# MLPs and output projections with 512-wide moving weights and stationary activations

## The chip, the cores and the metric

One core of a Trainium2 chip runs the whole kernel. The metric is the device time of one execution in microseconds (us). The kernel before was timed three times: 2537.08, 2537.50 and 2537.93 us, median 2537.5 us. The profile was taken from one more execution.

## What is computed

A trunk of two layers on 256 tokens of 2048 channels, all float32 (`SEQ = 256`, `D_MODEL = 2048`, `D_FF = 8192`). Cut to what this change touches:

```python
def squared_relu_mlp(h, w_up, w_down):
    u = h @ w_up                              # 2048 -> 8192
    return jnp.square(jax.nn.relu(u)) @ w_down  # 8192 -> 2048

# layer 0: attention and state-space heads share one input projection, then
x = x + concat([y_attn, y_ssd]) @ w_out       # 2048 -> 2048
x = x + squared_relu_mlp(rms_norm(x), w_up[0], w_down[0])
# layer 1: RWKV-7 time mixing, r, k, v projections and a scan over the tokens, then
x = x + (y * g) @ w_o                         # 2048 -> 2048
x = x + squared_relu_mlp(rms_norm(x), w_up[1], w_down[1])
```

Every large product is computed to float32 accuracy from two rounded halves of each operand: with x = xh + xl and w = wh + wl it is xh wh + xl wh + xh wl.

## The kernel before

**Layout.** The residual stream has channels on partitions: `x[d]` is [128 channels, 256 tokens], d = 0 to 15. The operand of a projection, `SA` or `SB`, is [128, 16, 512]: for each of 16 tiles of input channels (k) 256 columns of the rounded half and 256 of the rest.

**A unit** (`unit`, L372) is 128 outputs of a product with 2048 inputs. Its weights come in two loads of 512 KB (8 k tiles of 128x128 each; a load with its two halves is called a part below). ACT writes the rounded half `hi`, DVE the rest `lo`, three buffers each. Then TensorE makes two matmuls for each k, both with a tile of the weights as the stationary operand (`lhsT`): `hi` against all 512 columns of `X[:, k]`, `lo` against the first 256. The sum stands in one PSUM bank `pu` (two in turn) as two halves of 256 columns, which a reader adds.

**The MLP** (`mlp`, L515) makes 16 units of the up projection for a quarter c of the hidden channels, squares them into the other operand tile (ACT and DVE: `eb`, `u`, `uw`, `ut`, `split`), and then 16 units of the down projection, which DVE adds to `x[d]` in two steps. That is done for c = 0 to 3. 1/rms of the tokens multiplies `u`; it is made from squares that are summed over the tiles in `acc`, by matmuls and eleven short DVE steps (`token_rstd`). The last three tiles of the down projection of layer 0 (`'end': 3`) are left to the next stage (`mixer1_in`, steps `rest`).

**Output projections.** The first half of `w_out` (the attention heads) for 7 of the 16 tiles (`'early': 7`) and the first half of `w_o` for all 16 tiles (`o0a` to `o15a` in `PRM['order']`), and its second half for three of them (`+0a` to `+2a`), are multiplied within the mixers, among the work of the heads. There `feed` (L426) issues them: three matmuls of 256 columns for each k, again with the weights stationary. What is left follows in `out_proj` (L1029), which adds with DVE (`xT<-xT,pu`) and, for `w_o`, with POOL what the mixer had made of the first half (`xT<-xT,RY`).

**What sets the order.** Within the mixers a planner (`Streams`) issues the operations of many short programs in the order in which its rough costs let them start. In `out_proj` and `mlp` the framework's own scheduler orders the instructions of every engine. On the chip each engine works its list in order; loads of weights are issued by SP, the moves of the residual stream (`xd`, `out`) by POOL.

Of the kernel before, what the change touches and what calls it, by code (L numbers as in the profile page):

```python
# [97 lines left out]
def _heads(v):  # L98
    """a column to a head, on the first 64 partitions"""
    return np.concatenate([v.reshape(-1, HD).T, np.zeros((HD, D // HD), np.float32)], 0)  # L100


def layout(inp):
    a = {k: np.asarray(v) for k, v in inp.items()}
    o = {}
    o["xT"] = np.ascontiguousarray(a["x"][0].T.reshape(NK, P, L).transpose(1, 0, 2))
# [13 lines left out]
    o["w_out"] = _units(a["ev_w_out"][0][orow])  # L120
    for l in range(2):
        o[f"w_up{l}"] = _units(a["w_up"][l])
        o[f"w_dn{l}"] = np.ascontiguousarray(
            a["w_down"][l].reshape(4, NK, P, NK, P).transpose(0, 3, 2, 1, 4))
    for n in ("w_r", "w_k", "w_v", "w_o"):
        o[n] = _units(a["od_" + n][0])
    o["w1"] = np.ascontiguousarray(a["od_w1"][0].reshape(NK, P, 96).transpose(1, 0, 2))
# [31 lines left out]
# ---------------------------------------------------------------- interleaving  # L159
# [31 lines left out]
PRM = {'order': ['l0a', 'v0a', 'v0b', 'l1a', 'k3a', 'k3b', 'v1a', 'v1b', 'l2a', 'k4a', 'k4b', 'k5a', 'k5b', 'k6a', 'l3a', 'v2a', 'v2b', 'k6b', 'k7a', 'k7b', 'v3a', 'l4a', 'k8a', 'v3b', 'k8b', 'v4a', 'l5a', 'v4b', 'k9a', 'v5a', 'k9b', 'l6a', 'v5b', 'k10a', 'k10b', 'v6a', 'l7a', 'v6b', 'k11a', 'k11b', 'v7a', 'l8a', 'v7b', 'k12a', 'v8a', 'l9a', 'v8b', 'k12b', 'v9a', 'v9b', 'k13a', 'k13b', 'l10a', 'k14a', 'k14b', 'v10a', 'v10b', 'l11a', 'k15a', 'k15b', 'v11a', 'l12a', 'v11b', 'v12a', 'l13a', 'v12b', 'o0a', 'l14a', 'o1a', 'v13a', 'v13b', 'v14a', 'v14b', 'l15a', 'o2a', 'o3a', 'o4a', 'o5a', 'o6a', 'o7a', 'v15a', 'v15b', 'o8a', 'o9a', 'o10a', 'o11a', 'o12a', 'o13a', 'o14a', '+0a', '+1a', '+2a', 'o15a'], 'diff': 1.244, 'pool': 1000.0, 'b1p': 0.04, 'end': 3, 'step2': 1, 'w_blocks': -0.744, 'lat0P': 0.227, 'order0': [0, 12, 1, 2, 13, 14, 3, 4, 5, 15, 16, 24, 6, 17, 25, 7, 18, 19, 8, 20, 9, 21, 22, 26, 27, 10, 11, 23, 28, 29, 30, 31], 'm_attn1': -0.099, 'early': 7, 'm_gate': 0.043, 'm_norm_lo': 0.079, 'm_ssd': -0.022, 'pr': [3, 4], 'hid': [4, 7, 10], 'step1': 4, 'w_split_l': 0.571}  # L191
ORDER = 'v0a v0b l0a l1a k3a k3b v1a l2a v1b k4a k4b k5a k5b v2a l3a v2b k6a k6b k7a k7b v3a l4a v3b k8a k8b v4a l5a v4b k9a k9b v5a l6a v5b k10a k10b v6a l7a v6b k11a k11b v7a l8a v7b k12a k12b v8a l9a v8b k13a k13b v9a l10a v9b k14a k14b v10a l11a v10b k15a k15b v11a l12a v11b v12a l13a v12b o0a v13a l14a v13b o1a v14a l15a v14b o2a o3a v15a v15b o4a o5a o6a o7a o8a o9a o10a o11a o12a o13a o14a o15a +0a +1a +2a +3a'
ORDER = ORDER.split()

# [94 lines left out]
class Part:  # L289
    """Some k tiles of a unit, a 128-wide output tile of a projection. tiles: where the halves of the  # L290
    weights come to stand if the feed shall only split them; ready: the events that X[:, k] (the tiles) wait for"""
    def __init__(self, unit, h, src, X=None, n=8, m=P, k0=0, end=16, tiles=None, ready=None, bank=None):
        self.unit, self.key, self.src, self.X, self.n, self.m = unit, unit + (h,), src, X, n, m
        self.k0, self.end, self.tiles, self.ready, self.bank = k0, end, tiles, ready, bank


class Turns:
    """Tiles of a pool, n to a name, in turn"""
# [11 lines left out]
# ---------------------------------------------------------------- the program  # L310

class Trunk:
# [4 lines left out]
    # -- small helpers ---------------------------------------------------  # L317
# [24 lines left out]
    def mm(self, out, lhsT, rhs, start=True, stop=True):  # L342
        return self.nc.tensor.matmul(out, lhsT, rhs, start=start, stop=stop)  # L343
# [8 lines left out]
    def split(self, dst, src):  # L352
        """dst F32R [.., 512]: the rounded value and what it leaves, exactly"""
# [3 lines left out]
    def rsqrt(self, pool, v, shape, tag):  # L357
        """v f32 SBUF (any compact shape) -> 1/sqrt(v), Newton from the exponent trick"""
# [11 lines left out]
    # -- a 128-wide output tile of x @ W: [128, 512] in PSUM, the sum of its  # L370
# [1351 lines left out]
```

## Time and profile before

| what | value |
|---|---|
| median of three runs | 2537.5 us |
| span of the profiled execution | 2551.5 us |
| TensorE (PE) busy | 2477.5 us, 97% |
| weight loads (PEld) busy | 2181.3 us, 85% |
| DVE, ACT, POOL busy | 68%, 51%, 21% |
| memory traffic, mean | 163 GB/s |
| projection of layer 0 | from about 309 us |
| MLP of layer 0 | about 382 to 1106 us |
| r, k, v and the scan of layer 1 | about 1106 to 1757 us |
| rest of `w_o`, then MLP of layer 1 | about 1757 to 1817 us, then to 2547 us |

The profiled execution took 14 us (0.55%) longer than the median of the runs; its own rows are used for durations. In a timeline row the first number is the start in us from the span's start, the second how long it took; "x2" are two instructions merged into one row; in brackets stands how long the engine was idle before and which instruction released it. A matmul's own duration contains the time in which it drains through the array, so durations of neighbours overlap; the distance from start to start tells the rate.

### The profile page before, as it was taken

Reading aid. Unit: us, or ns where it says so; the run is one execution under the profiler, and the core shown is the slowest. Engines: PE = TensorE matmul, PEld = TensorE weight load, DVE = VectorE, ACT = ScalarE, POOL = GpSimd, SP = SyncE. Lnnn points to the kernel's source line nnn. Section 1 sums busy time; section 2 is a strip of 40 time slices with the busy share of each in tenths; the row PEclk is TensorE's granted clock in tenths of the full one; section 3 lists DMA queues with packets and bytes.
Section 4 is the critical chain, followed back from the end, with each engine's and each line's share of the span. In section 5 each row is a group of like instructions: output and inputs, shape, how many; then the busy total and the mean of one; then the engine's idle time right before and its main releaser. Section 6 shows DMA issues by size and latency. Waiting matters only on the chain. (4 is left out here: it accounts for less than half of the span.)

```text
span 2551.5 us, 45990 instructions
## 1 busy us (share of the span) xinstructions
PE 2477.5 (97%) x17612; PEld 2181.3 (85%) x17612; DVE 1738.2 (68%) x3287; ACT 1306.5 (51%) x2398; POOL 527.2 (21%) x933
## 2 busy tenths in 40 slices
PE   8999999999999999979999999999899999999999
PEld 7988988888888888879998888788688888888887
DVE  7888876656656656679876767667665565665665
ACT  5455555435445345556656566555453453453543
POOL 3443200000000000046455656552200000000000
PEclk9999999999999999989999999899999999999999
DMA  5433455555555555634442323334455555555554
GB/s 193 141 108 109 151 187 182 187 185 188 184 189 184 188 184 188 209 113 164 162 153 93 108 95 106 97 108 171 145 190 186 187 184 188 185 188 185 189 194 162
DMA packets 130348, 415.27 MB, mean 163 GB/s; under 512 B 23600, under 2 KB 26288, under 8 KB 130128
## 3 DMA queue, kind: packets, MB, share of 16 engines
q1 hardware_dynamic: 128160, 406.44, 46.9%
q0 software_dynamic: 1968, 5.90, 0.6%
q8 instruction: 138, 2.26, 0.3%
q14 instruction: 82, 0.67, 0.1%
HBM read 407.56 MB, written 4.72 MB: 162 GB/s over the span
## 5 line engine op out<-in xcount | busy, mean ns | idle before, releaser
L322 DVE TENSOR_TENSOR lo<-wt,hi 128x1024 fp32r<-128x1024 f32 (+2 forms) x895 | 937.4, 1054 | 529.6 <-ACT hi L319 511.8
L319 ACT ACTIVATE hi<-wt 128x1024 fp32r<-128x1024 f32 (+2 forms) x945 | 813.6, 873 | 818.3 <-PE pu L343 786.7
L343 PE MATMUL pu<-SA,hi 128*128 128x512 f32 (+2 forms) x4184 | 1162.0, 349 | 18.2 <-ACT SA L319 8.0
L343 PE MATMUL pu<-SB,hi 128*128 128x512 f32 (+2 forms) x3304 | 1003.1, 366 | 4.0 <-POOL SB L322 2.2
L343 PE MATMUL pu<-SA,lo 128*128 128x256 f32 (+1 forms) x3168 | 895.8, 283 | 0.3 <-DVE lo L322 0.3
L343 PEld LDWEIGHTS pu<-SA,hi 128*128 128x128 f32 (+1 forms) x4184 | 724.8, 191 | 135.2 <-ACT hi L319 9.7
L343 PE MATMUL pu<-SB,lo 128*128 128x256 f32 x2752 | 775.7, 282 | 1.7 <-DVE lo L322 1.6
L343 PEld LDWEIGHTS pu<-SB,hi 128*128 128x128 f32 (+1 forms) x3304 | 587.0, 190 | 115.6 <-POOL SB L322 2.6
L343 PEld LDWEIGHTS pu<-SA,lo 128*128 128x128 f32 (+1 forms) x3168 | 603.6, 191 | 1.2 <-DVE lo L322 0.5
L343 PEld LDWEIGHTS pu<-SB,lo 128*128 128x128 f32 x2752 | 522.6, 190 | 2.5 <-DVE lo L322 2.3
L1694 POOL DMA_DIRECT2D out<-xT x16 | 8.7, 544 | 708.0 <-DVE xT L322 708.0
L1661 POOL DMA_DIRECT2D xd<-xh x13 | 7.2, 554 | 696.5 <-DVE xh L322 696.5
L322 DVE TENSOR_TENSOR xh<-xh,pu 128x256 f32<-128x256 f32 x164 | 69.2, 422 | 53.7 <-PE pu L343 51.1
L322 DVE TENSOR_TENSOR xT<-xT,pu 128x256 f32<-128x256 f32 x154 | 64.8, 421 | 47.9 <-PE pu L343 45.3
L322 POOL TENSOR_TENSOR lo<-wt,hi 128x512 fp32r<-128x512 f32 (+1 forms) x50 | 69.1, 1387 | 66.3 <-ACT hi L319 62.2
L322 POOL TENSOR_TENSOR xt<-Nb,X 128x60 f32<-128x60 f32 (+14 forms) x240 | 74.7, 311 | 28.4 <-DMA Nb<-dn 12.1
L322 POOL TENSOR_TENSOR X<-X,xt 128x60 f32<-128x60 f32 (+14 forms) x240 | 74.2, 309 | 16.4
L319 ACT ACTIVATE uv<-ps_c,n 64x64 f32<-64x64 f32 x128 | 39.5, 309 | 53.0 <-PE ps_c L343 40.3
L322 POOL TENSOR_TENSOR SB<-st,SB 128x256 fp32r<-128x256 f32 x44 | 49.3, 1135 | 43.8 <-ACT SB L319 31.4
L340 DVE SCALAR_TENSOR_TENSOR uw<-u,rb 128x256 f32<-128x256 f32 x128 | 54.5, 425 | 4.4
L340 DVE SCALAR_TENSOR_TENSOR st<-dx,vec,xh 128x256 f32<-128x256 f32 x80 | 53.3, 700 | 2.0 <-POOL SB L322 2.0
L322 DVE TENSOR_TENSOR u<-pu,eb 128x256 f32<-128x256 f32 x128 | 53.6, 418 | 0.0
(310 smaller groups left out, 2073.2 us busy)
## 6 DMA issues: line engine op xcount, KB each, us to landing
wt<-in_w_up SPq DMA_DIRECT2D x256, 512.0 KB
wt<-in_w_dn SPq DMA_DIRECT2D x256, 512.0 KB
wt<-in_w_in SPq DMA_DIRECT2D x64, 512.0 KB
wt<-in_w_out SPq DMA_DIRECT2D x32, 512.0 KB
wt<-in_w_k SPq DMA_DIRECT2D x32, 512.0 KB
wt<-in_w_v SPq DMA_DIRECT2D x32, 512.0 KB
wt<-in_w_o SPq DMA_DIRECT2D x32, 512.0 KB
wt<-in_w_r SPq DMA_DIRECT2D x26, 512.0 KB
```

The source lines that it names most:

```text
L319: return self.nc.scalar.activation(out=out, in_=in_, func=func, **kw)
L322: return (eng or self.nc.vector).tensor_tensor(out=out, in0=a, in1=b, op=op)
L340: return self.nc.vector.scalar_tensor_tensor(out=out, in0=a, scalar=s, in1=b, op0=op0, op1=op1)
L343: return self.nc.tensor.matmul(out, lhsT, rhs, start=start, stop=stop)
L1661: spill = lambda d, e=nc.gpsimd: e.dma_start(out=xd[:, d, :], in_=x[d])
L1694: store = lambda d: nc.gpsimd.dma_start(out=ap["out"][:, d, :], in_=x[d])
```

## The change

Weights become the moving operand and activations the stationary one. `wide` replaces `unit`: a block is 512 outputs for all 256 tokens in two PSUM banks, one for each 128 tokens. A part is now 2 k tiles of 512 outputs (the same 512 KB, 4 KB in a row on each partition). For each k and each half of the tokens there are three matmuls of 512 columns: xh against `hi`, xh against `lo`, xl against `hi`. Outputs therefore come with tokens on partitions, and the residual stream is kept so: `x` is [128, 2, 2048]. What needs channels on partitions again is transposed by TensorE: the hidden activations of the MLP (`u`, four 128x128 transposes for each 128 tokens of a block), and x before each normed product (`features`). 1/rms now scales the rows of `u` in its `Relu`, and the squares are summed by ACT (`accum_out`). Parts inside the mixers (`tok=True`) have 256 outputs and 4 k tiles, with six matmuls of 256 columns for each k. The three tiles left over at the end of layer 0 are gone; x is loaded once more, with tokens on partitions (2 MB).

```diff
-    def unit(self, src, X, h0=0):
-        ps = self.psu("pu", 2, [P, 512])
-        for h in range(h0, 2):
...
-                self.mm(ps, hi[:, kk, :], X[:, k, :], start=k == 8 * h0, stop=False)
-                self.mm(ps[:, L:], lo[:, kk, :], X[:, k, 0:L], start=False, stop=k == 15)
+    def wide(self, src, X, ps, parts=range(8)):
+        for i in parts:
+            wt, hi, lo = (self.wp(n, 3, [P, 8 * P], t).rearrange("p (k m) -> p k m", m=512)
+                          for n, t in (("wt", F32), ("hi", F32R), ("lo", F32R)))
+            nc.sync.dma_start(out=wt, in_=src[:, 2 * i:2 * i + 2, :])
+            self.act(hi, wt)
+            self.sub(lo, wt, hi.bitcast(F32))
+            for t in range(2):
+                q = slice(t * P, t * P + P)
+                for kk in range(2):
+                    k = 2 * i + kk
+                    xh, xl = X[:, k, q], X[:, k, L:][:, q]
+                    self.mm(ps[t], xh, hi[:, kk], i == parts[0] and kk == 0, False)
+                    self.mm(ps[t], xh, lo[:, kk], False, False)
+                    self.mm(ps[t], xl, hi[:, kk], False, i == parts[-1] and kk == 1)
+    def features(self, db, x, emit):
+        for h in range(2):
+            ps = self.pst.tile([P, 512], F32, name="pt")
+            for q in range(2):
+                k = 4 * db + 2 * h + q
+                for t in range(2):
+                    self.tp(ps[:, q * L + t * P:q * L + (t + 1) * P], x[:, t, k * P:(k + 1) * P], self.c["ident"])
...
     def mlp(...)
             for c in range(4):
-                for f in range(16):
-                    ps = self.unit(ap[f"w_up{l}"][c * 16 + f], X)
-                    u = self.ev.tile([P, L], F32, name="u")
-                    self.usum(ps, u)
-                    self.stt(w, u, 0.0, ALU.max, rb, ALU.mult)
-                    self.act(t, w, AF.Square)
-                    self.split(U[:, f, :], t)
-                for d in range(NK if c < 3 else end):
-                    ps = self.unit(ap[f"w_dn{l}"][c, d], U)
-                    self.add(x[d], x[d], ps[:, 0:L])
-                    self.add(x[d], x[d], ps[:, L:])
+                for f in range(4):
+                    ps = [self.psy.tile([P, 512], F32, name="py") for _ in range(2)]
+                    self.wide(ap[f"w_up{l}"][c * 4 + f], X, ps)
+                    for t in range(2):
+                        u = ev.tile([P, 512], F32, name="u")
+                        self.act(u, ps[t], AF.Relu, scale=r[:, t:t + 1])
+                        pt = self.pst.tile([P, 512], F32, name="pt")
+                        for q in range(4):
+                            self.tp(pt[:, q * P:(q + 1) * P], u[:, q * P:(q + 1) * P], self.c["ident"])
+                        s = ev.tile([P, 4, P], F32, name="us")
+                        self.act(s, pt.rearrange("p (a b) -> p a b", b=P), AF.Square)
+                        hi = U[:, 4 * f:4 * f + 4, t * P:(t + 1) * P]
+                        self.act(hi, s)
+                        self.sub(U[:, 4 * f:4 * f + 4, L + t * P:L + (t + 1) * P], s, hi.bitcast(F32))
+                for d in range(4):
+                    ps = [self.psy.tile([P, 512], F32, name="py") for _ in range(2)]
+                    self.wide(ap[f"w_dn{l}"][c, d], U, ps)
+                    for t in range(2):
+                        self.add(x[:, t, blk(d)], x[:, t, blk(d)], ps[t])
...
     def out_proj(...)
+        for d in range(4):
+            o = [x[:, t, d * 512:(d + 1) * 512] for t in range(2)]
             if part is not None:
-                self.add(x[d], x[d], part[:, d, :], self.nc.gpsimd if d < NK - 1 else None)
+                for t in range(2):
+                    self.tt(..., part[:, 2 * d:2 * d + 2, t, :], ALU.add, self.nc.gpsimd)
+            if 2 * d >= ahead:
+                ps = [self.psu("pu", 2, [P, 512]) for _ in range(2)]
+                self.wide(w[d], Y, ps, range(4 if 2 * d < early else 0, 8))
+                for t in range(2):
+                    self.add(o[t], o[t], ps[t])
             finish(d)
...
-PRM = {'order': [..., 'o13a', 'o14a', '+0a', '+1a', '+2a', 'o15a'], 'end': 3, 'early': 7, ...}
+PRM = {'order': [..., 'o7a', 'o7b', '+0a', '+0b', '+1a', '+1b'], 'early': 4, ...}
```

The next two lists are TensorE's in the MLP of layer 0, where a unit or a block ends and the next begins. Before, one unit (bank `pu0_119`) is followed by the next (`pu1_236`) with no other work between them (`SB` is the activations, `hi` and `lo` the halves of the weights):

```order
L343 MATMUL pu0_119<-SB_74,hi0_126 128x512
L343 MATMUL pu0_119<-SB_74,lo0_127 128x256
L343 MATMUL pu1_236<-SB_74,hi1_164 128x512
L343 MATMUL pu1_236<-SB_74,lo1_165 128x256
L343 MATMUL pu1_236<-SB_74,hi1_164 128x512
```

Now, at the end of a block of the up projection (banks `py_4566` and `py_4567`), the eight transposes of its `u` into `pt` stand among the first matmuls of the next block (`py_4710`):

```order
L350 MATMUL py_4567<-hi2_237,SA_73 128x512
L350 MATMUL py_4567<-lo2_238,SA_73 128x512
L350 MATMUL py_4567<-hi2_237,SA_73 128x512 x2
L350 MATMUL py_4567<-lo2_238,SA_73 128x512
L350 MATMUL py_4567<-hi2_237,SA_73 128x512
L353 MATMUL pt_4690<-cst_78,u_4688 128x128 x4
L350 MATMUL py_4710<-hi0_124,SB_74 128x512
L350 MATMUL py_4710<-lo0_125,SB_74 128x512
L353 MATMUL pt_4701<-cst_78,u_4699 128x128 x4
L350 MATMUL py_4710<-hi0_124,SB_74 128x512 x2
```

All matmuls of a block now have 512 columns; four transposes come right behind the block's last matmul, four more two matmuls later.

The second place is POOL's list at the end of the scan of layer 1, where x comes back from memory and the last pair of heads is finished (`yc`, `ysq`, `RY`). Before:

```order
L322 TENSOR_TENSOR RY<-ysq_12863,g_12228 128x256 [waits Pool_49]
L1693 DMA xT<-xd 128x1024 [waits DMAHW5_49,DMAHW4_49,DMAHW6_49,DMAHW3_49,DMAHW7_49,DMAHW2_49,PE_49]
L1693 DMA xT<-xd 128x1024 x3
L322 TENSOR_TENSOR yc_12859<-yc_12859,gy_12888 128x256 [waits DVE_49,Activation_49]
L322 TENSOR_TENSOR ysq_12863<-ysq_12863,bv_11978 128x256 [waits Activation_49,Pool_49]
L322 TENSOR_TENSOR RY<-ysq_12863,g_12512 128x256 [waits Pool_49]
L322 TENSOR_TENSOR xT<-xT,RY 128x256 [waits DMASW5_49,DVE_49]
```

Now:

```order
L1679 DMA xu<-xd 128x2x512 [waits DMAHW5_49,DMAHW6_49,DMAHW1_49,DMAHW7_49,DMAHW0_49,PE_49]
L1679 DMA xu<-xd 128x2x512 x3
L329 TENSOR_TENSOR xu<-xu,RY 128x512 [waits DMASW5_49]
L329 TENSOR_TENSOR xu<-xu,RY 128x512
L329 TENSOR_TENSOR xu<-xu,RY 128x512 [waits DMASW6_49,Activation_49]
L329 TENSOR_TENSOR yc_11357<-yc_11357,gy_11386 128x256 [waits DVE_49,Activation_49]
L329 TENSOR_TENSOR xu<-xu,RY 128x512
L329 TENSOR_TENSOR ysq_11361<-ysq_11361,bv_10476 128x256 [waits Activation_49,Pool_49]
L329 TENSOR_TENSOR RY<-ysq_11361,g_11010 128x256 [waits Pool_49]
L329 TENSOR_TENSOR xu<-xu,RY 128x512 [waits DMASW7_49,Activation_49]
```

Three additions of 512 columns, which wait for x to land from memory (`DMASW5`, `DMASW6`), now stand ahead of the last pair's `yc`, and one more between its steps.

## Rows read from the trace of the kernel before

**Rows 1.** The page: TensorE's busy time, share of the span, instructions, and other engines'.
```profile
PE 2477.5 (97%) x17612; PEld 2181.3 (85%) x17612; DVE 1738.2 (68%) x3287; ACT 1306.5 (51%) x2398; POOL 527.2 (21%) x933
```

**Rows 2.** Two stretches: length, busy time of PE, PEld, DVE, ACT, POOL, granted clock, DMA.
```profile
382.00:1106.00 724.00, 723.82 (x4142) 629.11 (x4140) 441.89 (x608) 346.66 (x483) 7.73 (x15) 1.00 0.54 187
...
1817.00:1831.00 14.00, 10.69 (x51) 8.88 (x51) 9.76 (x25) 4.86 (x8) 1.87 (x3) 0.88 0.33 118
```

**Rows 3.** Groups by shape, TensorE: count | busy us, mean ns of one | idle before.
```profile
L343 PE MATMUL pu<-SA,lo 128*128 128x256 f32 x3152 | 890.4, 283 | 0.3 <-DVE lo L322 0.3
L343 PE MATMUL pu<-SB,hi 128*128 128x512 f32 x2200 | 778.2, 399 | 0.9 <-DVE xT L322 0.9
L343 PE MATMUL pu<-SB,lo 128*128 128x256 f32 x2720 | 766.6, 282 | 1.2 <-DVE lo L322 1.2
L343 PE MATMUL pu<-SA,hi 128*128 128x512 f32 x2152 | 762.1, 399 | 7.4 <-DVE xT L322 7.4
L343 PE MATMUL pu<-SA,hi 128*128 128x256 f32 x2000 | 391.4, 295 | 0.9 <-ACT SA L319 0.7
L343 PE MATMUL pu<-SB,hi 128*128 128x256 f32 x1040 | 212.9, 301 | 0.0
```

**Rows 4.** Timeline of TensorE in the MLP of layer 0, 27 pairs apart.
```profile
399.85 0.40 PE L343 MATMUL pu<-SA,hi 128*128 128x512 f32 x1
...
409.39 0.40 PE L343 MATMUL pu<-SA,hi 128*128 128x512 f32 x1
```

**Rows 5.** The same in the first up projection of layer 1, 18 pairs apart.
```profile
1850.12 0.39 PE L343 MATMUL pu<-SB,hi 128*128 128x512 f32 x1
...
1856.36 0.39 PE L343 MATMUL pu<-SB,hi 128*128 128x512 f32 x1
```

**Rows 6.** The same in the first mixer, four k tiles of three matmuls apart.
```profile
134.76 0.40 PE L343 MATMUL pu<-SA,hi 128*128 128x256 f32 x2
...
136.20 0.40 PE L343 MATMUL pu<-SA,hi 128*128 128x256 f32 x2
```

**Rows 7.** The same at four transposes among matmuls, in the scan.
```profile
1714.47 0.60 PE L346 MATMUL ps_y<-cst,yc 128*64 128x128 f32 x4
1714.83 0.48 PE L343 MATMUL pu<-SB,hi 128*128 128x256 f32 x2
```

**Rows 8.** Timeline, all engines: a part's last matmul and what ACT starts behind it.
```profile
400.45 0.28 PE L343 MATMUL pu<-SA,lo 128*128 128x256 f32 x1
...
400.99 1.06 ACT L319 ACTIVATE hi<-wt 128x1024 fp32r<-128x1024 f32 x1 [1.49 <-PE pu L343]
```

**Rows 9.** Groups by shape, ACT.
```profile
L319 ACT ACTIVATE hi<-wt 128x512 fp32r<-128x512 f32 x396 | 235.3, 621 | 48.6 <-PE pu L343 29.1 <-DMA wt<-in_w_k 7.8 <-DMA wt<-in_w_r 7.2
...
L319 ACT ACTIVATE eb<-pu 128x256 f32<-128x256 f32 x128 | 46.9, 367 | 0.0
...
L319 ACT ACTIVATE th<-ps_a,dv 128x256 f32<-128x256 f32 x16 | 7.6, 473 | 13.5 <-PE ps_a L343 13.5
```

**Rows 10.** TensorE's waits from 1756 to 1832 us: total us, times, longest.
```profile
PE pu L343 <- DVE xT L322: 8.3, 9, 0.9
PE ps_m L343 <- DVE acc L322: 3.0, 1, 3.0
```

**Rows 11.** Timeline of POOL from 1740 us.
```profile
1747.45 2.18 POOL L1693 DMA_DIRECT2D xT<-xd  x4 [4.37 <-PE ps_c L343]
1755.14 0.61 POOL L322 TENSOR_TENSOR yc<-yc,gy 128x256 f32<-128x256 f32 x1 [5.50 <-DVE gy L340]
...
1774.21 0.73 POOL L322 TENSOR_TENSOR xT<-xT,RY 128x256 f32<-128x256 f32 x1 [13.93 <-DVE xT L322]
1777.62 1.65 POOL L322 TENSOR_TENSOR xT<-xT,RY 128x256 f32<-128x256 f32 x1 [2.68 <-DVE xT L322]
```

**Rows 12.** DMA issues by group: count, KB each, median us from issue to landing.
```profile
xT<-xd POOLq DMA_DIRECT2D x4, 512.0 KB, 7.5
out<-xT POOLq DMA_DIRECT2D x16, 128.0 KB, 2.2
```

More of the change, by code (lines that the diff above doesn't have):

```diff
@@ L289, with __init__ @@
 class Part:
-    def __init__(self, unit, h, src, X=None, n=8, m=P, k0=0, end=16, tiles=None, ready=None, bank=None):
+    def __init__(self, unit, h, src, X=None, n=8, m=P, k0=0, end=16, tiles=None, ready=None, bank=None, tok=False):
         self.unit, self.key, self.src, self.X, self.n, self.m = unit, unit + (h,), src, X, n, m
+        self.tok = tok
         self.k0, self.end, self.tiles, self.ready, self.bank = k0, end, tiles, ready, bank
@@ L421, in even, with mean_square @@
+    def mean_square(self, v):
+        self.nc.vector.tensor_reduce(out=v, in_=self.ssq, axis=mybir.AxisListType.X, op=ALU.add)
+        self.ts(v, v, 1.0 / D, ALU.mult, EPS, ALU.add)
     def even(self, t):
@@ L1013, in partial @@
             def partial(d):
[L1014 to L1016 removed]
+                yield eW(("sum", "o", d), *(("xt", i) for i in range(4)))
+                t = yield eD(0.6)
+                o = xt[:, :, d * 256:(d + 1) * 256]
+                self.add(o, o, sums["o", d].rearrange("p (t m) -> p t m", t=2))
                 done[("out", "o", d)] = t
@@ L1072, in mixer1_in @@
                       unit("g", 0, ap["g1"][0], 5) + unit("g", 1, ap["g1"][1], 5)]
-            parts = [Part(("d", d), q, ap["w_dn0"][3, d][:, q * 8:q * 8 + 8, :], SB, k0=q * 8)
-                     for d in range(end, NK) for q in range(2)]
+            parts = []
             pr = prm('pr', (2, 2))
@@ L1091, in part @@
                 return (low(j) if n == "l" else half("v", j, q, SA, ready=lambda k: [("mix", 3, k)]) if n == "v" else
-                        half("k", j, q, SB) if n == "k" else out("o", j, 0) if n == "o" else out("o+", j, 1))
-            parts += [part(t) for t in prm('order', ORDER)]
+                        half("k", j, q, SB) if n == "k" else out("o", j, 0, q) if n == "o" else out("o+", j, 1, q))
+            parts += [part(t) for t in PRM['order']]
             last = {4: ("w", 0), 5: ("a", 0), 2: ("g", 1), 3: ("r", NK - 1)}
-            def rest(i):
-                d = end + i
-                yield eW(("sum", "d", d))
-                t = yield eD(0.34)
-                self.add(h[:, d, 1:], h[:, d, 1:], sums["d", d][:, 0:L])
-                done[("out", "d", d)] = t
-                done[("squares", d)] = yield eA(0.31)
-                self.act(sq[d % 2], h[:, d, 1:], AF.Square)
-                if d < NK - 1:
-                    yield eD(0.34)
-                    self.add(self.acc, self.acc, sq[d % 2])
-                yield eS(0.45, t)
-                spill(d, nc.sync)
-                if d - 2 in scaled:
-                    yield eA(0.4, 0)
-                    self.act(h[:, d - 2, 1:], h[:, d - 2, 1:], AF.Copy, scale=self.vcol("g_mix1", d - 2))
             def rstd(_):
@@ L1119, in rstd @@
                 nc.gpsimd.memset(h[:, :, 0:1], 0.0)
-                yield eW(("squares", NK - 1))
-                yield from self.rstd_steps([self.acc] + ([sq[1]] if end < NK else []), D, self.rb, pp, rt, "n1")
+                v = rt.tile([P, 2], F32, name="n1v")
+                yield eD(0.14, 0)
+                self.mean_square(v)
+                y = yield from self.rsqrt_steps(rt, v, "n1")
+                yield from self.expand_steps(y, self.rb, pp, rt, "n1")
             def either(dve, pool, cap=0.35, t=None):
@@ L1188, in mixer1_in @@
             with tc.manual_schedule():
-                if end < NK:
-                    sch.stage(rest, NK - end)
-                else:
-                    done[("squares", NK - 1)] = 0.0
                 sch.stage(rstd, 1)
@@ L1687, in build @@
[L1687 to L1705 removed]
+                    self.squares(x, d)
@@ new lines, in build @@
+            self.mixer1(SA, SB)
+            with tc.tile_pool(name="x1", bufs=1) as xp, tc.tile_pool(name="ev1", bufs=2) as self.ev2, \
+                    tc.tile_pool(name="pt1", bufs=2, space=PSUM) as self.pst, tc.tile_pool(name="py1", bufs=4, space=PSUM) as self.psy:
+                x = xp.tile([P, 2, D], F32, name="xu")
+                for d in range(4):
+                    nc.gpsimd.dma_start(out=x[:, :, blk(d)], in_=xd[:, :, blk(d)])
+                self.out_proj(ap["w_o"], SA, x, normed(x, "g_ffn1", SB), self.RY.rearrange("p (u a) b -> p u a b", a=2), ahead=self.ahead)
+                self.mlp(1, x, SB, SA, lambda d: nc.gpsimd.dma_start(out=ap["out"][:, :, blk(d)], in_=x[:, :, blk(d)]))
```

230 lines of the change are left out of this document (87 added, 143 removed).

## The prediction

> **What bounds the kernel now.** I read the page's busy times first, then the stretches, then TensorE's timeline inside them. TensorE is busy for 2477.5 of the 2551.5 us of the profiled execution, DVE for 68%, ACT for 51% [rows 1]. In the 724 us of the MLP of layer 0 TensorE is busy for 723.8 us at a granted clock of 1.00, so the full level of 2.4 GHz, while DMA is at 0.54 of its time [rows 2]. The matmuls are almost never waited for: the groups of 512 columns stood idle for 8.3 us altogether [rows 3]. So nothing that the change takes from DVE, ACT or the number of loads shortens an MLP; only the rate at which TensorE works through columns does, and what is put among them. Busy time doesn't tell that rate, since durations overlap: starts do. 27 pairs (512 and 256 columns) start within 409.39 - 399.85 = 9.54 us, 353.3 ns a pair [rows 4]. In the first up projection of layer 1 18 pairs take 6.24 us, 346.7 ns [rows 5]; no other long stretch of the MLPs has that. In the mixers, where the same 768 columns are three matmuls of 256, four k tiles take 1.44 us, 360 ns each [rows 6]. Outside the MLPs TensorE waits at two seams: after layer 0's MLP, and between the scan of layer 1 and its MLP, where it waits 8.3 us for DVE's additions to `xT`, 3.0 us for `acc` [rows 10], and then works below the full level for a while (0.88 over 14 us [rows 2]).
>
> **The change part by part**, against the profiled execution.
>
> *Matmuls of the products.* The columns that are streamed stay the same: before, 4352 matmuls of 512 and 8912 of 256 [rows 3]; after, counted over the program's list, 6576 of 512 and 4464 of 256; both are 4,509,696 columns. What falls is the number of matmuls and weight loads, by 2224. What is that worth? No row shows 512 following 512. From 360 = 768b + 3a and 353.3 = 768b + 2a [rows 4, 6], a matmul costs 6.7 ns besides its columns (0.443 ns each), and one of 512 takes 233.3 ns. With the pace of rows 5 in place of rows 4, a is 13.3 ns, a column 0.417 ns (one cycle of 2.4 GHz), and 512 take 226.7 ns. If all is proportional to columns, it is 353.3 x 2/3 = 235.6 ns. From below, the bare columns at 0.417 ns are 213.3 ns. I take 232 ns, near the value of rows 4, which holds nearly everywhere, and a little towards rows 5, where nothing but pace differs. Before: 4352 x 353.3 + 4560 triples of 120 ns each matmul, that is (8912 - 4352)/3 x 360 = 1537.7 + 547.2 = 2084.9 us. After: 6576 x 232 + 4464 x 120 = 1525.6 + 535.7 = 2061.3 us. **-23.6 us**; at 226.7 ns -58.4, at 235.6 ns 0, at 213.3 ns -146.
>
> The Trainium skill ("TensorE: Matmul & The Clock Gate", section "Back-to-back issue gap") gives N/2.4 + 2.5 ns from matmul to matmul, 215.7 ns for 512 columns; by it the saving would be 131 us. The trace so far disagrees: by the same rule a pair would take 324.9 ns, and the rows have 353.3 and 346.7.
>
> *Transposes.* New on TensorE: 256 for `u` (2 MLPs x 16 blocks x 8) and 96 for x (3 x 32). None of 128x128 inside an MLP is in the trace; the scan's four take 1714.83 - 1714.47 = 0.36 us between matmuls [rows 7]. That makes (256 + 96)/4 x 0.36 = 31.7 us; the last eight of layer 0 stand where TensorE waits anyway (-0.7). **+31.0 us**; nothing covers them, since TensorE is the engine that is full. From below 27 us (were the switch free), from above 0.60 us a group, the whole duration in that row: 53 us.
>
> [...] The row says 0.36 us for four, so I keep that.
>
> *Waits for `u`.* The first four transposes wait for an activation that can run while the block's last six matmuls go on. The second four wait for the one on the bank that ends with the block: ACT starts 0.54 us after a last matmul's start [rows 8], and a 512-column activation takes 0.62 us, plus 0.1 for its scale (473 against 367 ns) [rows 9]: 1.26 us. Until TensorE gets there it has 0.23 (that matmul) + 0.36 + 2 x 0.23 = 1.05 us of work. The wait is 0.2, with handing over 0.25 us, 32 times: **+8 us**, between 0 and the 34 us of the rival below. Behind the waiting transposes the whole of TensorE's list stands.
>
> *From the scan to layer 1's MLP.* Gone: the nine waits for `xT` and that for `acc`, 11.3 us [rows 10], and perhaps the low clock after them, 0.12 x 14 = 1.7 us. New: POOL's three additions of 512 columns ahead of the last pair's `yc`. They need x from memory, asked for at 1747.45 and there 7.5 us later [rows 11, 12], and take 2 x 0.73 us alone or 2 x 1.65 beside a busy DVE [rows 11]: `yc` comes 4 to 10 us after the 1755.14 of before, and what hangs on it is `RY`, the last k tiles of `+0b`, and TensorE's list behind it. The parts of `w_o` give TensorE cover for some of that; I count 5 us. Then the first transposes of x wait for two more POOL additions (3 us), and three blocks for a DVE addition (0.4 us each). **-3 us**, between -11 and +8.
>
> *The rest.* The last store is 512 instead of 128 KB: 7.5 against 2.2 us to land [rows 12], of which I take **+2** (0 to 5.3). Where layer 0's MLP ends the three left-over tiles are finished earlier, and no TensorE work stood behind them; additions and squares of 512 columns make the chain there **0.5 us** longer. Less work of DVE and ACT in the MLPs, 2 MB of x and smaller pieces of `w_o` cost nothing: DMA is at half its time, and TensorE's work covers them.
>
> Sum: -23.6 + 31.0 + 8 - 3 + 2 + 0.5 = +14.9 us. The runs' median lies 14 us under the profiled execution; I add the difference to it: 2537.5 + 15 = **2552 us**.
>
> **The rivals.**
>
> *A fixed price per matmul* (13.3 ns). For it: with rows 5 and 6 the column comes out at exactly one cycle. Against it: rows 5 is rare. 226.7 ns: -58.4 in place of -23.6, so 2552 - 35 = 2517 us.
>
> *Columns alone count.* Then fewer loads are worth nothing. For it: 353.3 ns splits 2 to 1 in rows 4, as the columns do. Against it: rows 6, where one more matmul costs 6.7 ns. 2552 + 24 = 2576 us.
>
> *The full rate.* The extra time of a 512 comes from the 256 beside it, whose load isn't covered, and goes with it: 213.3 ns, 6576 x 18.7 ns less, 123 us: 2429 us. Against it: a stationary of 128 columns is loaded for every matmul in rows 4 to 6 alike. The rule of 215.7 ns in the Trainium skill, same section as above, is this rival, with 16 us less of a gain.
>
> *ACT stands in the way of the transposes* (slower). If ACT starts a part's rounding of 1.06 us [rows 8] just before the second `u`, all of TensorE waits that much longer at each of 32 blocks: +34 us, 2586 us. It decides once `hi` precedes `u` in ACT's list or the block's end comes while `hi` runs. Against it: in the list both `u` stand together, ahead of the rounding that the block's end releases.
>
> **How the numbers follow.** About 0.2% (5 us) is what a measurement of this kernel can tell from no change. Forecast 0.42, with its own range 2538 to 2568 us (230 to 234 ns, and the seam's bounds); fixed price 0.19; columns alone 0.20; full rate 0.07; ACT in the way 0.12. Faster: 0.19 + 0.07 + 0.04 of the forecast's lower end = 0.30. Within 0.2%: 0.14, all from the forecast's lower end. Slower: the 0.24 that is left of it, + 0.20 + 0.12 = 0.56. The range leaves out the full rate and the far ends: 2511 to 2590 us.
>
> **What would show it.** In the MLPs the distance between starts of `py` matmuls: 232 ns bears the first term, 227 or 236 the first two rivals. Four transposes of `u` in 0.36 us, and an idle time of about 0.25 us before every second group, ended by ACT. At the scan's end `yc` on POOL behind three additions, with TensorE waiting a few us. I am wrong above all if 512 columns behind 512 run below 229 ns: then the kernel is faster.

## The result, and the profile after

The changed kernel takes 2556.36 us (median of 4 runs, 2551.5 to 2558.34), the kernel before in the same measuring 2537.72. The ratio on record is 1.0062, 95% interval 1.0041 to 1.0084, so 0.6% slower; ratios are given as they stand on record, and differ by about 0.1% from the quotient of two medians (here 1.0073). On a second chip it was 1.0043 (1.0021 to 1.0065). The forecast was 2552 us.

The profiled executions stand the other way round (span 2549.7 us after, 2551.5 before). The granted clock of the scan of layer 1, where the change touches only the pieces of `w_o`, goes with that: one row of each over the same 590 us, columns as in [rows 2].

The kernel before, with 0.95:

```profile
1150.00:1740.00 590.00, 565.81 (x6018) 502.07 (x6018) 446.04 (x1144) 353.46 (x869) 340.29 (x714) 0.95 0.37 120
```

The changed kernel, with 0.99:

```profile
1150.00:1740.00 590.00, 563.88 (x6160) 501.41 (x6158) 456.09 (x1162) 363.35 (x888) 354.90 (x726) 0.99 0.39 126
```

The third column from the right is the granted clock. It differs from execution to execution there (0.94 in a run of e7, 0.98 in e5), and 0.04 of 590 us is up to 24 us; runs of before went from 2532 to 2564 us over all measurings. So the kernels are compared by ratios of many runs, and their traces by stages outside the scan.

A part of this is no accident of one execution. In the measuring of e5 the mean clock of the whole execution was 0.9860 over 29 runs of the kernel before and 0.9889 over 12 of the changed kernel, and within the 29 runs 0.01 of clock goes with 19 us. By that, an estimate, the changed kernel gained some 5 us which no term of the prediction has. In the traces of before, e1, e7 and e9 TensorE's clock is at its lower level of 1.2 GHz for 14 to 38 us around 1620 to 1650 us; in e11, and in eight of the nine traces of kernels with moving weights, it is not. Why is not shown. The kernel before and the changed kernel there:

```profile
1610.00:1660.00 50.00, 47.52 (x500) 40.09 (x500) 30.97 (x94) 25.98 (x67) 25.82 (x67) 0.80 0.29 92
```

```profile
1610.00:1660.00 50.00, 46.30 (x583) 39.04 (x578) 38.94 (x114) 31.50 (x80) 32.05 (x77) 1.00 0.31 97
```

The page's line of engines answers to [rows 1]: 1896 matmuls and as many weight loads fewer, and TensorE as busy as before.

```profile
PE 2478.6 (97%) x15716; PEld 2077.9 (81%) x15716; DVE 1535.7 (60%) x2680; ACT 1280.7 (50%) x2194; POOL 512.1 (20%) x905
```

The stretch of the MLP of layer 0 answers to the first row of [rows 2], the groups by shape to [rows 3]. TensorE has no idle time at all there; DVE went from 441.89 to 349.38 us, which can have bought nothing, as TensorE was full before too.

```profile
382.00:1106.00 724.00, 724.00 (x3182) 580.73 (x3181) 349.38 (x331) 331.13 (x380) 2.17 (x3) 1.00 0.61 185
```

```profile
L350 PE MATMUL py<-hi,SB 128*128 128x512 f32 x2048 | 649.7, 396 | 0.0
...
L350 PE MATMUL py<-lo,SB 128*128 128x512 f32 x1024 | 404.8, 395 | 0.0
...
L350 PE MATMUL pu<-SA,hi 128*128 128x256 f32 x1952 | 375.1, 291 | 0.2
...
L353 PE MATMUL pt<-cst,u 128*128 128x128 f32 x256 | 40.1, 279 | 0.0
```

The pace is read from starts, as in [rows 4]. TensorE's timeline in the first down projection, 39 matmuls of 512 columns apart: 9.10 us, **233.3 ns each**.

```profile
540.34 0.39 PE L350 MATMUL py<-lo,SB 128*128 128x512 f32 x1
...
549.44 0.40 PE L350 MATMUL py<-lo,SB 128*128 128x512 f32 x1
```

At the end of an up block stand the two groups of transposes of `u`; the same view, every row:

```profile
403.01 0.63 PE L350 MATMUL py<-hi,SA 128*128 128x512 f32 x2
403.48 0.40 PE L350 MATMUL py<-lo,SA 128*128 128x512 f32 x1
403.71 0.41 PE L350 MATMUL py<-hi,SA 128*128 128x512 f32 x1
403.96 0.60 PE L353 MATMUL pt<-cst,u 128*128 128x128 f32 x4
404.31 0.48 PE L350 MATMUL py<-hi,SA 128*128 128x512 f32 x1
404.63 0.40 PE L350 MATMUL py<-lo,SA 128*128 128x512 f32 x1
404.90 0.66 PE L353 MATMUL pt<-cst,u 128*128 128x128 f32 x4
405.31 0.70 PE L350 MATMUL py<-hi,SA 128*128 128x512 f32 x2
405.85 0.39 PE L350 MATMUL py<-lo,SA 128*128 128x512 f32 x1
```

Four transposes take 404.31 - 403.96 = 0.35 us from first start to the next matmul's start, as in [rows 7]. But from that matmul's start to the next it is 404.63 - 404.31 = 0.32 us in place of 0.233, so a part of the group's time stands in the row behind it. A group costs 0.35 + 0.09 = **0.44 us**. The second group shows the wait: it starts 0.27 us after the matmul ahead of it where 0.233 were due, and takes 0.41 in place of 0.35 to the next start, together **0.10 us**. All 64 groups of the trace, 32 of each kind, have these distances within 0.01 us. The wait is too short to be listed among TensorE's waits; its weight loads have it, ended by ACT's `u`:

```profile
404.90 0.42 PEld L353 LDWEIGHTS pt<-cst,u 128*128 128x128 f32 x4 [0.31 <-ACT u L326]
```

At the scan's end POOL's timeline answers to [rows 11], and the waits of TensorE from 1740 to 1812 us (total, times, longest) to [rows 10].

```profile
1745.77 2.93 POOL L1679 DMA_DIRECT2D xu<-xd  x4 [6.29 <-PE ps_c L350]
1754.64 4.26 POOL L329 TENSOR_TENSOR xu<-xu,RY 128x512 f32<-128x512 f32 x3 [5.95 <-DMA xu<-xd]
1758.86 0.61 POOL L329 TENSOR_TENSOR yc<-yc,gy 128x256 f32<-128x256 f32 x1
```

```profile
PE ps_y L353 <- POOL yc L329: 3.5, 1, 3.5
PE pt L353 <- POOL xu L329: 2.3, 2, 1.8
PE pt L353 <- DVE xu L329: 0.5, 2, 0.3
```

`yc` starts behind the three additions, at 1758.86, as their list had it; TensorE waits 3.5 us for it and 2.8 for x, where before it waited 8.3 + 3.0. The end: the last matmul (TensorE), the addition (DVE) and the store (POOL).

```profile
2543.89 0.40 PE L350 MATMUL py<-hi,SA 128*128 128x512 f32 x1
```

```profile
2544.32 0.69 DVE L329 TENSOR_TENSOR xu<-xu,py 128x512 f32<-128x512 f32 x1 [0.72 <-PE py L350]
```

```profile
2545.30 0.69 POOL L1681 DMA_DIRECT2D out<-xu  x1 [21.69 <-DVE xu L329]
```

From the last matmul's start to the span's end it is 5.9 us; before it was 5.7. The larger store landed in 4.0 us, not 7.5.

The stages, in us from start to start of their first or last matmuls in the timelines of four executions (the kernel before again and the changed kernel again are runs of the next section; e1 and e5). In before, three tiles' last quarter, 17 us of work behind the MLP of layer 0, is counted to that MLP, which begins 2000 pairs ahead of its last; and the 3.0 us for which TensorE waits for `acc` [rows 10] fall into its MLP of layer 1.

| stage | before | before, e1 | after | after, e5 |
|---|---|---|---|---|
| start to MLP of layer 0 | 379.6 | 379.6 | 380.7 | 381.6 |
| MLP of layer 0 | 726.1 | 724.4 | 735.5 | 735.5 |
| seam to the mixer of layer 1 | 9.9 | 9.8 | 10.1 | 10.1 |
| mixer, scan, seam to the MLP of layer 1 | 701.7 | 696.2 | 684.3 | 689.7 |
| MLP of layer 1 | 728.6 | 729.4 | 733.3 | 733.3 |
| end | 5.7 | 5.6 | 5.9 | 5.8 |

The MLPs got 4 to 11 us longer each (7 to 11 without before's wait for `acc`), the mixer and seams 6 or more shorter.

### The profile page after: what moved, and what is told of

Read it like the earlier page. It is cut to its first block, busy times and chain, and to the rows that moved or that the text cites. A ratio compares the mean times of both kernels' runs of the same rounds, so it can differ in the third digit from the quotient of the medians.

```text
span 2549.7 us, 41137 instructions
## 1 busy us (share of the span) xinstructions
PE 2478.6 (97%) x15716; PEld 2077.9 (81%) x15716; DVE 1535.7 (60%) x2680; ACT 1280.7 (50%) x2194; POOL 512.1 (20%) x905
## 5 line engine op out<-in xcount | busy, mean ns | idle before, releaser
L350 PE MATMUL py<-hi,SB 128*128 128x512 f32 x2048 | 649.7, 396 | 0.0
L350 PE MATMUL py<-hi,SA 128*128 128x512 f32 x2048 | 649.4, 396 | 0.0
L350 PEld LDWEIGHTS py<-hi,SA 128*128 128x128 f32 x2048 | 382.7, 188 | 91.5
L350 PE MATMUL py<-lo,SB 128*128 128x512 f32 x1024 | 404.8, 395 | 0.0
L350 PE MATMUL py<-lo,SA 128*128 128x512 f32 x1024 | 404.5, 395 | 0.0
L350 PE MATMUL pu<-SA,hi 128*128 128x256 f32 (+1 forms) x1984 | 383.0, 292 | 10.2 <-ACT SA L326 6.8
L350 PEld LDWEIGHTS pu<-SA,hi 128*128 128x128 f32 (+1 forms) x1984 | 305.5, 190 | 24.1 <-ACT SA L326 7.2
L350 PE MATMUL pu<-SA,lo 128*128 128x256 f32 (+1 forms) x992 | 281.2, 283 | 0.3 <-DVE lo L329 0.2
L350 PEld LDWEIGHTS pu<-SA,lo 128*128 128x128 f32 (+1 forms) x992 | 187.9, 189 | 1.2 <-DVE lo L329 1.0
L350 PEld LDWEIGHTS pu<-SB,hi 128*128 128x128 f32 (+1 forms) x640 | 97.3, 186 | 8.7 <-POOL SB L329 2.8
```

## The experiments

Ratios are to runs of the kernel before that were made beside them on the same chip, with 95% intervals.

**e1: the kernel before again.**

> The kernel before once more, for a trace beside those of this chip. Open is why the profiled execution of before took 14 us more than its runs. Theory: the mixers, which the change leaves as they are, ran slower in it: a granted clock of 0.95 where the changed kernel shows 0.98 (600 us) and 119.6 ns in place of 118.3 for a matmul of 256 columns; a pair in the MLPs stays at 353 ns. Then this execution takes about 2537 to 2540 us, with the clock near 0.98 between 1131 and 1740 us and pairs at 353 ns. Rival: the MLPs ran slower in it, and at 2537 us pairs start every 350 ns (4352 x 3.2 ns = 14 us); then the changed kernel's 233.4 ns for 512 columns is no gain at all.

One run, 2546.88 us (median of before on that chip 2544.36, 2538.7 to 2549.3). The theory had 2537 to 2540 us and a clock near 0.98 in the scan; the clock was 0.96 there, so it failed in both. Nor did the rival's faster pairs show: the MLPs had pairs of 353.3 ns nearly throughout again, and 256 columns in the mixers took 120 ns again. So the pace of before's pairs, on which the sum rests, is the ordinary one, and the 120 ns belong to the program. That left a question: the same code of the mixers runs at 118.3 ns in the changed kernel. Its rows stand under e9.

**e2: no transposes of `u`.** The down projections multiply other numbers then.

```
-  for q in range(4):
-      self.tp(pt[:, q * P:(q + 1) * P], u[:, q * P:(q + 1) * P], ident)
-  self.act(s, pt.rearrange(...), AF.Square)
+  self.act(s, u.rearrange(...), AF.Square)
```

> The changed kernel without the 256 transposes of u: ACT squares u from SBUF where it read the transposes' bank, everything else stays; what is left out is the turn of the hidden units onto partitions, so the products of the down projections are others. Theory from the trace of the changed kernel: the 64 groups take 0.354 us each, the second of each pair 0.09 more in waiting: 22.7 + 3 = 26 us less, about 2531 us. By the prediction's terms: 23 + 8 = 31 us less, 2525. Rival: the matmuls themselves are what got slower, and the transposes stand in slack: no change, 2556. By 0.275 us for each transpose it would be 70 us less, 2486.

2525.44 us, 0.9926 of before (0.9910 to 0.9942): 1.2% under the changed kernel's 1.0043, some 30 us. The first and last matmul of the MLP of layer 0 without the transposes:

```profile
382.46 0.40 PE L350 MATMUL py<-hi,SA 128*128 128x512 f32 x1
...
1102.55 0.39 PE L350 MATMUL py<-hi,SB 128*128 128x512 f32 x1
```

and in the changed kernel:

```profile
380.67 0.39 PE L350 MATMUL py<-hi,SA 128*128 128x512 f32 x1
...
1116.17 0.39 PE L350 MATMUL py<-hi,SB 128*128 128x512 f32 x1
```

720.1 against 735.5 us; in layer 1 it is 717.7 against 733.3. Together 31.0 us: exactly the prediction's 23 + 8, though split otherwise (64 x 0.44 = 28 for the transposes, 32 x 0.10 = 3 for the waits). My expectation of 26 us was too low, because it still took 0.354 for a group. Without the transposes the changed kernel would be faster than before: they are the loss.

The Trainium skill ("TensorE: Matmul & The Clock Gate", "Part 4: PE-mode transpose") has about 275 ns for a bf16 transpose of 128x128 within a kernel; here, in float32, the mean duration in the groups above, 279 ns, is near it, but the four overlap, start 109 ns apart, and a group of them costs 0.44 us: durations are no price.

**e3: every 512 cut into two 256.**

```
-  self.mm(ps[t], xh, hi[:, kk], ...)
+  for n in range(2):
+      self.mm(ps[t][:, c], xh, hi[:, kk, c], ...)      # c: columns n * 256 ...
```

> The changed kernel with each of its 6576 moving-weight matmuls of 512 columns cut into two of 256 with the same stationary operand, so twice the matmuls and weight loads and the same columns. Theory (columns alone count, since the trace of the changed kernel has 233.4 ns for 512 and 118 for 256 columns): 2 x 117 to 118 ns, 0 to +17 us, 2556 to 2573. The prediction's price of 6.7 ns a matmul: +44 us, 2600. The fixed price of 13.3 ns: +87 us, 2644.

2562.43 us, 1.0077 (1.0056 to 1.0097). 78 matmuls of 256 columns apart:

```profile
540.06 0.63 PE L350 MATMUL py<-hi,SB 128*128 128x256 f32 x4
...
549.16 0.63 PE L350 MATMUL py<-hi,SB 128*128 128x256 f32 x4
```

9.10 us again, 116.7 ns each. The MLPs are 738.5 and 737.2 us long, 3 and 4 more than the changed kernel's. Twice the matmuls and loads cost 1 ns apiece: columns alone count at this place, the load of 128 stationary columns is hidden behind 256 moving ones. The prices of 6.7 and 13.3 ns a matmul have fallen.

**e4: up projections as before, the rest as changed.** 1/rms squared goes into the down projection's addition.

```
-  ps = [self.psy.tile(...) for _ in range(2)]; self.wide(w_up, X, ps); transposes of u
+  ps = self.unit(ap[f"w_up{l}"][c * 16 + f], X)            # pairs of 512 and 256 columns
...
-  self.add(x[:, t, blk(d)], x[:, t, blk(d)], ps[t])
+  self.stt(x[:, t, blk(d)], ps[t], r2[:, t:t + 1], ALU.mult, x[:, t, blk(d)], ALU.add)
```

> The changed kernel with the up projections as before (stationary weights, 128 outputs at a time, pairs of 512 and 256 columns; no transposes of u) and the rest as changed: moving weights in down and output projections, tokens on partitions; 1/rms squared is applied at the down projections' addition. Theory: the transposes and their waits go, 26 us; 2048 pairs at 353.3 ns in place of 3072 matmuls at 233.5 add 6: about 2537 us, as before within 4 us. Rival (pairs at the pace of 346.7 to 350 ns in an ordinary run): 2523 to 2530. Rival (the loss is in the token layout of the residual, not in the transposes of u): above 2550.

2526.74 us, 0.9930 (0.9912 to 0.9949): 18 us under before where the theory had them level, and so faster than both kernels; the rival with faster pairs held. In most of its up projections 18 pairs take what they take in [rows 5]:

```profile
2399.99 0.39 PE L350 MATMUL py<-SB,hi 128*128 128x512 f32 x1
...
2406.23 0.39 PE L350 MATMUL py<-SB,hi 128*128 128x512 f32 x1
```

6.24 us, 346.7 ns a pair. Six of its eight up stretches have that pace, which is rare in before, two have 353 ns; in e8 below, at the same place of the weights, it is four and four. The token layout as such loses nothing.

**e5: the changed kernel again**, beside e6 to e8.

> The changed kernel itself once more, on the chip of the next three, so that each can be set against it. Theory (the loss is the transposes): it stands 0.4 to 0.9% over before; the run without transposes of u stood at 0.9926 of before, so the transposes are then worth 1.1 to 1.6%, of which 26 us (1.0%) is what the trace shows and the rest the difference between chips.

2557.53 us, 1.0043 (1.0021 to 1.0065), as expected.

**e6: the additions of RY on DVE.**

```
-  ... part[:, 2 * d:2 * d + 2, t, :], ALU.add, self.nc.gpsimd)
+  ... part[:, 2 * d:2 * d + 2, t, :], ALU.add)
```

> The changed kernel with the eight additions of RY to x (after the scan) on DVE in place of POOL; nothing else. Theory: POOL then finishes the last pair's yc as soon as DVE has its scale, so TensorE's wait of 3.7 us before the last four transposes of the scan goes, and the waits of 0.7 and 1.9 us for xu at the first transposes of x shrink to under 0.5 each; DVE has 0.4 of its time free there. 4 to 6 us less than the changed kernel. Rival: the additions stand in DVE's list among the steps of the last pair's scale and wait there for x from memory, so that yc comes as late as on POOL: 0, or up to 3 us more.

2557.26 us, 1.0043 (1.0025 to 1.0061): no change. DVE's timeline, between two small steps of the last pair's scale:

```profile
1758.07 0.16 DVE L344 TENSOR_SCALAR gy<-gs 128x4 int32<-128x4 int32 x1
1761.55 0.69 DVE L329 TENSOR_TENSOR xu<-xu,RY 128x512 f32<-128x512 f32 x1 [3.32 <-DMA xu<-xd]
1762.16 0.15 DVE L329 TENSOR_TENSOR gt<-gy 128x4 f32<-128x4 f32 x1
```

and the waits of its TensorE from 1740 to 1820 us:

```profile
PE ps_y L353 <- POOL yc L329: 4.5, 1, 4.5
PE pt L353 <- DVE xu L329: 0.5, 2, 0.3
```

The rival was right: DVE stands 3.3 us before x lands, in the middle of the chain that makes `yc`. That wait grows from 3.5 to 4.5 us while the 2.3 us for `xu` go; the 1.3 us left over are too little for the runs to show.

**e7: the kernel before, two wide matmuls and then two narrow ones.**

```
-  for kk in range(8):
-      self.mm(ps, hi[:, kk, :], X[:, k, :], ...)
-      self.mm(ps[:, L:], lo[:, kk, :], X[:, k, 0:L], ...)
+  for kk in range(0, 8, 2):
+      for i in range(2): self.mm(ps, hi[:, kk + i, :], X[:, k + i, :], ...)
+      for i in range(2): self.mm(ps[:, L:], lo[:, kk + i, :], X[:, k + i, 0:L], ...)
```

> The kernel before, with the order of matmuls in the MLPs' units changed: the two of 512 columns of two k tiles, then their two of 256, in place of one and one. Same matmuls, same loads. Theory (a column costs 0.4557 ns wherever a matmul follows one of its own width, and the alternation of widths gives before its two paces of 353.3 and 346.7 ns a pair): 700 ns for two pairs all through, 4352 x 3.3 = 14 us less than before, and runs that lie closer together. Rival (the two paces have nothing to do with the order): both paces again, no change within 5 us. Rival (a change of width costs): half as many changes, 346.7 ns or less, 29 us less.

2527.13 us, 0.9931 (0.9908 to 0.9954). 13 groups of two and two apart:

```profile
540.15 0.63 PE L343 MATMUL pu<-SB,hi 128*128 128x512 f32 x2
...
549.21 0.63 PE L343 MATMUL pu<-SB,hi 128*128 128x512 f32 x2
```

9.06 us, 348.5 ns a pair, and so in both MLPs. 4352 x (353.3 - 348.5) = 21 us, about the 19 measured. The theory had the direction (14 us), not the size; the rival's 29 us, for a price of each change of width, were not reached either. The same matmuls and loads in another order take 5 ns less a pair, so these 5 ns of before's 353 come from how the two widths follow each other.

**e8: e4 and e6 together.**

> Up projections as before, moving weights in down and output projections (0.993 of before on its first chip), with the additions of RY on DVE as well. Theory: the two gains add, 0.9910 to 0.9920 of before. Rival: DVE, which has more to do in this version, hides nothing there: 0.993 as without.

2523.52 us, 0.9905 (0.9873 to 0.9936); the interval takes in e4's 0.9930, so whether DVE's additions give anything here is not shown.

**e9 and e10: 32 bytes more in front of the weights' tiles.** Both kernels' first tile of rounded weights begins at a place of SBUF that the sizes of the tiles ahead of it set: at 64 modulo 128 bytes in before, at 96 in the changed kernel, whose new tile `ssq` has 32 bytes. The same two lines were put into each:

```
+  self.pad = kp.tile([P, 8], F32, name="pad")
+  nc.gpsimd.memset(self.pad, 0.0)
   cst = self.cst = kp.tile([P, NCONST[0]], F32, name="cst")
```

> The kernel before with one tile of 32 bytes a partition more ahead of the constants, so that the weights' tiles begin at 32 in place of 0 modulo 64 bytes, where they lie in the changed kernel (its tile for sums of squares has 32 bytes). Nothing else. Open is why a matmul of 256 columns in the mixers, whose code is the same, takes 120 ns in every trace of before and 118.2 in every trace of the changed kernel. Theory (where the weights' tiles begin sets it): 118.2 in the mixers here too, 4560 x 1.5 = 7 us less, and the pairs of the MLPs mostly at 346.7 ns as in the run with up projections as before, up to 4352 x 6.6 = 28 us less: 0.986 to 0.997 of before. Rival (it comes from the program's other parts): 120 ns and 353 ns stay, 1.000.

> The changed kernel with the same tile of 32 bytes, so that its weights' tiles begin at 0 modulo 64 bytes, as in the kernel before. Theory (where they begin sets the pace of narrow matmuls with stationary weights): 120 ns for 256 columns in the mixers, 4464 x 1.5 = 7 us more than the changed kernel; the 512-column matmuls with moving weights stay at 233.4 ns. Rival (moving operands are read faster from there): under 230 ns for 512 columns, 6576 x 4 = 26 us less or more. Rival (it comes from elsewhere): the same as the changed kernel, 1.004 to 1.006 of before.

Before with 32 bytes: 2539.06 us, 0.9983 (0.9960 to 1.0005). In the mixers 118.3 ns, as the theory had it; the pairs kept 353 ns nearly everywhere, so the large part of its gain failed, and the interval takes in no gain at all. The mixers' matmuls of 256 columns in two timelines; the kernel before, 186 apart, 120.0 ns:

```profile
1216.01 0.40 PE L343 MATMUL pu<-SB,hi 128*128 128x256 f32 x2
...
1238.33 0.40 PE L343 MATMUL pu<-SA,hi 128*128 128x256 f32 x2
```

before with 32 bytes, 219 apart, 118.3 ns, which is the changed kernel's pace as well:

```profile
1238.89 0.40 PE L343 MATMUL pu<-SA,hi 128*128 128x256 f32 x2
...
1264.80 0.40 PE L343 MATMUL pu<-SB,hi 128*128 128x256 f32 x2
```

The changed kernel with 32 bytes: **2528.21 us, 0.9922 (0.9898 to 0.9946)**, some 30 us less than without. My theory had it 7 us slower; the rival of a faster moving operand was the one that held. 39 matmuls of 512 columns apart:

```profile
540.67 0.39 PE L350 MATMUL py<-lo,SB 128*128 128x512 f32 x1
...
549.60 0.39 PE L350 MATMUL py<-lo,SB 128*128 128x512 f32 x1
```

8.93 us, 229.0 ns. 6144 x 4.3 = 26 us, and the MLPs are 722.6 and 720.1 us long, 12.9 and 13.2 less. Nothing of the change is undone in it: the transposes and their 31 us are all there.

**e11 and e12: the same place for the kernel before, and for the mixture.** e11 has a tile of 64 bytes in before, e12 one of 32 in e8; in both the first rounded weights begin at 0 modulo 128, as in e10.

> The kernel before with one tile of 64 bytes a partition more, so that the weights' tiles begin where they do in the changed kernel with 32 bytes more (97408 for the first hi: 0 modulo 128; before 64, changed kernel 96). The changed kernel fell from 1.0043 to 0.992 of before by that shift, its 512-column matmuls from 233.4 to 228.9 ns. Open is what the change costs with the weights in one place. Theory (where the weights begin sets the pace of both kernels alike; the change itself costs the transposes): pairs at 1.5 x 228.9 = 343.4 to 346.7 ns and 116 to 118 ns for 256 columns: 29 to 43 us and 8 to 15 us less, 0.978 to 0.985 of before, so 18 to 35 us faster than the changed kernel at the same place. Rival (only moving weights gain from the place): 353 ns for a pair, 0.995 to 1.000, and the changed kernel is the faster one there by 10 us.

> Up projections as before, moving weights in down and output projections, additions of RY on DVE (0.9905 of before), with the tile of 32 bytes, so that its weights' tiles begin at the same place (0 modulo 128). Theory: the 512-column matmuls with moving weights run at 228.9 ns and the pairs at 343 to 347, as in the other kernels of this place: 3500 x 4.5 = 16 us less, up to 7 more for the pairs, 0.981 to 0.985 of before: the fastest of all, or level with the kernel before at this place. Rival (pairs lose what the 512 gain): 0.990 as without.

e11: 2542.92 us, 0.9982 (0.9961 to 1.0003). 28 pairs apart in its MLP:

```profile
540.14 0.40 PE L343 MATMUL pu<-SB,hi 128*128 128x512 f32 x1
...
550.04 0.40 PE L343 MATMUL pu<-SB,hi 128*128 128x512 f32 x1
```

9.90 us, 353.6 ns; in the mixers, 177 matmuls apart, 20.06 us, 113.3 ns:

```profile
1211.92 0.39 PE L343 MATMUL pu<-SB,hi 128*128 128x256 f32 x2
...
1231.98 0.39 PE L343 MATMUL pu<-SA,hi 128*128 128x256 f32 x2
```

So the rival held: the alternating pairs, whose moving operand is the activations, don't gain from this place; 512 moving columns of weights do. The 113.3 ns are of one of the faster stretches: over the mixers of e10, e11 and e12 the mean is 115 to 116 ns, against 119.6 in before. For 4560 matmuls that would be some 18 us. Up to the MLP of layer 0 it shows (374.8 us in place of 379.6), but the runs as a whole got 5 us faster, 10 at most by the interval: the pace of the 256 columns is not passed on in full by the mixers.

e12: **2514.47 us, 0.9881 (0.9858 to 0.9905)**, the fastest of all; its theory overshot (0.981 to 0.985) because it gave the pairs a gain that they don't have: all eight up stretches run at 353 ns, where four of eight had 346.7 in e8 (1024 x 6.6 = 7 us).

What the two shifted kernels say of the change: at 96 modulo 128 the changed kernel stands at 1.0043 against 0.9983, **0.6% slower**; at 0 it stands at 0.9922 against 0.9982, **0.6% faster**. At both places the two intervals are apart.

## Why the prediction was right, step by step, and what it missed

The time came 4 us from the forecast, with errors that cancel.

- *What bounds the kernel*: held. TensorE is busy all through the MLPs, and what DVE and the loads were spared gave next to nothing (e3 shows it for loads directly).
- *Matmuls of the products*: **mis-sized**. "I take 232 ns, near the value of rows 4": it measured 233.3; 6576 x 1.3 = 9 us that the saving lost, so -15 in place of -24. Rows 4 and 6 by themselves gave the measured value, but by luck: the 6.7 ns a matmul behind it are refuted by e3. By e3's 1 ns, 2224 matmuls fewer are worth 2 us; most of the 15 come from widths that no longer alternate, as in e7 (4352 pairs at 353.3 ns against 768 columns at the pace of 233.3 for 512, 350.0 ns: 14 us). Against that, the mixers' untouched matmuls of 256 columns took 118.3 ns in place of 120, 4464 x 1.7 = 7 us that no term had, if the mixers pass it on, which e9 and e11 don't show.
- *Transposes*: mis-sized. 0.36 us a group is what [rows 7] show to the next matmul's start; the 0.09 us that this next matmul loses are not in it. 88 x 0.44 = 39 us in place of 31 (measured on the 64 groups of `u`; for the 24 of x it is taken over). The lower bound of 27 us has no row behind it, and no run shows a group at such a price.
- *Waits for `u`*: the place was right, the size 0.10 and not 0.25 us, 3 in place of 8 us: the cover was longer by the same 0.09 behind the first group, and ACT started 0.45, not 0.54 us behind the block's last matmul. With the transposes of `u` alone, 28 + 3, the prediction's 23 + 8 is hit as a sum (e2).
- *From the scan to layer 1's MLP*: POOL's list did what its order said; `yc` was waited for 3.5 us (5 predicted), x 2.8 (4 predicted), and the 11.3 us are gone: 6.3 us of new waits in place of some 9, so -5 where -3 was put. The low clock is not gone: 3.4 us of it stand near 1761 us, as before near 1825.
- *The rest*: the last store +0.2 in place of +2 us, the seam behind layer 0's MLP +0.2 in place of +0.5.

With the measured sizes the sum is -15 + 38 + 3 - 5 + 0 = +21 us (38: the transposes less what waited anyway), and +9 if the 7 us of the mixers and the 5 us of the higher clock count in full; the measurings have +18.6 and +11.

Of the rivals, the fixed price and the price per matmul are refuted by e3, ACT's rounding never stood in the way (0.10 us), and columns nearly alone is what counts at this place; that rival's 235.6 ns was too high because it took before's alternating pairs for pure columns. But e10 shows that the whole argument had a hidden condition. The prediction took the price of 512 columns from the kernel before, as if it were a constant of the chip. It is 233.3 ns where the diff happens to put the weights and 229.0 ns 32 bytes further, and that difference (26 us) is larger than the forecast's margin over before. The forecast's sign was right for a reason that its text doesn't contain. The rule of the Trainium skill that spoke for a large gain (same page as above, "Back-to-back issue gap", 215.7 ns for 512 columns, there the gap of an isolated matmul) holds at neither place; it is 13 and 18 ns too low here.

What stays open: which tile's place matters. The shift moves the constants and all working tiles behind it too; `SA` and `SB` stay. Only three places were tried, and the changed kernel not at 64. Nor is it settled what puts alternating pairs at 346.7 or 353 ns: before, e4, e8 and e9 have both in one execution, and e7 removes the choice.

## What to carry to other kernels

When TensorE is full, more columns per instruction may save little by themselves: here the loads of 128 stationary columns were hidden behind 256 moving ones already (1 ns a matmul in e3); what the new layout added to TensorE's list was paid in full, and a layout that needs no transposes (stationary weights up, moving weights down) took the gain without the price. Price an inserted group by the distance between two ordinary matmuls around it, counting the one behind it, not by its own durations or its first neighbour's start. And before a difference of half a per cent is ascribed to a change, shift its tiles by 32 bytes in both kernels: here that alone turned 0.6% slower into 0.6% faster.

## What the runs showed of the hardware that was not expected

| first rounded weights at, modulo 128 bytes | 256 columns, stationary weights, in the mixers | 512 columns, moving weights | alternating pair |
|---|---|---|---|
| 64 (before, e1) | 120.0 ns | - | 353.3, rarely 346.7 |
| 96 (changed kernel, e4, e8, e9) | 118.3 ns | 233.3 ns | 353.3, rarely 346.7 in e9, half in e8, mostly in e4 |
| 0 (e10, e11, e12) | 113.3 ns at best, 115 to 116 in the mean | 229.0 ns | 353.3 |

All at a granted clock of 1.00 in these stretches: the full level of 2.4 GHz, at which 512 columns at one a cycle would be 213.3 ns. In these kernels the pace of a matmul went with where the tiles lie, by 2% for 512 columns of moving weights and by 3% in the mean for 256, and two alternating widths were 5 ns slower than the same two grouped (e7).
